# State-space layer: silu and the decays' differences on ScalarE, exponentials in one run, more multiplies on VectorE, the gated norm in two parts

## The chip, the cores and the metric

One core of a Trainium2 chip runs the whole program. The metric is the device time in microseconds, the median of several runs. TensorE (PE) does the matmuls, with weight loads (PEld) beside them; VectorE (DVE), ScalarE (ACT) and GpSimd (POOL) do elementwise work; SyncE (SP) issues most of the DMAs.

## The reference

A trunk of two layers over 512 tokens of width 1024, all in f32. Layer 0 mixes by pooling and chunked attention, layer 1 by a Mamba-2 state-space layer; a mixture of experts follows each. The change is in layer 1's mixer:

```python
zxbcdt = h @ w_in                                   # 512x1024 by 1024x6176
z, xbc, dt = jnp.split(zxbcdt, ...)                 # 2048, 4096, 32 columns
conv = sum(xp[:, tap:tap + s] * conv_w[tap] for tap in range(4))
xbc = jax.nn.silu(conv + conv_b)
xs, Bm, Cm = jnp.split(xbc, ...)                    # 32 heads of 64; 8 groups, state 128
dt = softplus(dt + dt_bias);  x_dt = xs * dt
a_cs = cumsum(dt * -exp(A_log))                     # within a chunk
seg = exp(where(tril, a_cs[l] - a_cs[s], -inf))     # decay between two tokens
y_diag = einsum(Cm, Bm, seg, x_dt)
states = einsum(Bm, exp(a_cs[-1] - a_cs), x_dt)     # one state per chunk, scanned over chunks
y = y_diag + einsum(Cm, prev, exp(a_cs)) + xs * D_skip
g = (y * silu(z)) grouped by 8                      # 256 columns in a group
g = g * rsqrt(mean(g * g) + EPS) * norm_w
out = g @ w_out
```

## The kernel before

`odd_mixer` is the state-space layer. Its loop runs over the 8 groups `g`, with a ninth turn that finishes group 7. Tokens lie along the free axis (512), and are cut in 4 chunks of 128 for the scan (index `cq`).

In each turn PE runs six **dense blocks** of 24 matmuls, in the order `b`, `c`, `x0`, `x1`, `z0`, `z1`. A dense block multiplies the 1024 inputs by 128 columns of `w_in`, with operand and weight each split in a high and a low half (three products). The weights' halves are made two blocks ahead by `wsplit`: ACT copies the high half (L111), and a subtraction makes the low half (L112) on the engine that a string names in turn; for this layer the string is `LO["o"] = "GVV"`, so that every third block's low half is POOL's.

Behind a block of `b`, `c` or `x` comes `conv`: Identity with scale and bias on ACT (L1584), three taps on DVE (L1587), and silu as Tanh on ACT (L1590) with a multiply-add on DVE (L1591). `zgate` does the same for `z` (L1680, L1681). `decay(g, cq)` reads a row of cumulated logs by DMA into `lb`, takes four differences with a minimum on DVE (L1620), an Exp on ACT (L1622) and a mask multiply (L1623, alternately POOL and DVE) and leaves `ms`. `xtok` turns `x` by eight transposes on PE into `pxd` (L1637), multiplies by `dt` on DVE (`xdt`, L1640) and by the decay to the chunk's end on POOL (`xw`, L1643). One group later, `states` multiplies `xw` by `btk` (`pst`, L1651) behind the `b` block and scans the chunks (`prev`), `ymm` makes the outputs' two parts `pyd` (L1670, from `ms` and `xdt`) and `pyo` (L1674), and `assemble` joins them (`yy`, `yt` L1689, POOL's sum L1691, `gT` L1692), squares them and sums them into `gsum` (L1699, POOL). `gnorm` norms two groups at once, after each second turn: two matmuls (`pgn`, L1705), one step on DVE, Ln and Exp on ACT, three steps on DVE, a broadcast on POOL and a scaling of `gT` on DVE (L1721).

Between groups DVE also works on two vectors of the conditioning (`ada`, L202, 128x2048 a step), as many steps a group as `OFILL` says. A static scheduler orders each engine's instructions by priority and by what they need; no engine leaves its order at run time. After the mixer comes the output projection (`so`, L457 to L459), whose operands are `gT`.

Of the kernel before, what the change touches and what calls it, by code (L numbers as in the profile page):

```python
# [9 lines left out]
F32 = mybir.dt.float32  # L10
# [10 lines left out]
P = 128  # L21
# [37 lines left out]
HEAD = 1  # L59
NTMP = 3  # L60
TAIL = 2
FILL = (0, 1, 5, 0, 1, 0, 1, 1, 1, 2, 1, 0, 0, 1, 0, 5, 4, 0, 0, 1, 1, 1, 4, 0, 12)
OFILL = (4, 0, 5, 4, 4, 0, 3, 4)
LO = {"v": "V", "e": "VVG", "m": "V", "o": "GVV", "s": "VV"}
FPOOL = (0,)
# [11 lines left out]
def trunk_kernel(ctx, tc, x, c, ada_w, ada_b, norm1_w, norm2_w, mix_w_in, pool_w, pool_scale,  # L77
# [1377 lines left out]
    def odd_mixer(layer, prev):  # L1455
        with ExitStack() as es:
# [25 lines left out]
            with ExitStack() as es2:  # L1482
# [94 lines left out]
                def tmp(name):  # L1577
                    return gp.tile([P, T], F32, tag="tmp", name=name, bufs=NTMP)

                def conv(kind, ch, bufs, between=None):  # L1580

                    p = dense.next(between)
                    a = gp.tile([P, T], F32, tag=f"cv{kind}", name=f"cv{kind}{ch}", bufs=bufs)
                    S.activation(a, p, AF.Identity, bias=cb[:, ch:ch + 1], scale=cw[:, 3, ch:ch + 1])  # L1584
                    for tap in (2, 1, 0):
                        sh = 3 - tap
                        V.scalar_tensor_tensor(a[:, sh:], p[:, :T - sh], cw[:, tap, ch:ch + 1], a[:, sh:], op0=ALU.mult,  # L1587
                                               op1=ALU.add)
# [25 lines left out]
                def decay(g, cq):  # L1614

                    lb = gp.tile([P, 4, P], F32, tag="lb", name=f"lb{g}{cq}", bufs=2)
                    SP.dma_start(lb, dap(acd, (32 * cq + 4 * g) * P, [[0, P], [1, 4 * P]]))
                    ms = gp.tile([P, 4, P], F32, tag="ms", name=f"ms{g}{cq}", bufs=3)
                    for h in range(4):
                        V.tensor_scalar(ms[:, h, :], lb[:, h, :], acs[:, cq, 4 * g + h:4 * g + h + 1], 0.0,  # L1620
                                        op0=ALU.subtract, op1=ALU.min)
                    S.activation(ms, ms, AF.Exp)  # L1622
                    (V if cq % 2 else GP).tensor_mul(ms, ms, gs[g]["cbm"][:, cq, None, :].to_broadcast([P, 4, P]))  # L1623
                    gs[g]["ms", cq] = ms

                def xtok(g):
# [5 lines left out]
                    for c2 in range(2):  # L1632
# [5 lines left out]
                        for e in range(2):  # L1638
# [3 lines left out]
                            if cq < NT - 1:  # L1642
                                GP.tensor_mul(xw[:, cq], xdt[:, cq], dec[:, cq, hs, None].to_broadcast([P, 4, 64]))  # L1643

# [32 lines left out]
                def zgate(g, q):  # L1677
                    pz = dense.next()
                    z = gs[g]["z", q] = gp.tile([P, T], F32, tag="zt", name=f"zt{g}{q}", bufs=2)
                    S.activation(z, pz, AF.Tanh, scale=0.5)  # L1680
                    V.scalar_tensor_tensor(z, z, 1.0, pz, op0=ALU.add, op1=ALU.mult)  # L1681

                def assemble(g, q):
# [7 lines left out]
                    GP.tensor_add(y[:, P:], y[:, P:], t[:, P:])  # L1691
                    V.tensor_mul(gT[2 * g + q], y, d["z", q])  # L1692
                    if q == 0:
# [7 lines left out]
                def gnorm(g0):  # L1701
# [5 lines left out]
                    v = tmp(f"gv{g0}")  # L1707
                    V.tensor_scalar(v, p, 1.0 / 1024, EPS, op0=ALU.mult, op1=ALU.add)
                    y = tmp(f"gy{g0}")
                    S.activation(y, v, AF.Ln)  # L1710
                    S.activation(y, y, AF.Exp, scale=-0.5)
                    t = tmp(f"gt{g0}")
                    V.tensor_mul(t, y, y)
                    V.scalar_tensor_tensor(t, t, -0.25, v, op0=ALU.mult, op1=ALU.mult)
                    V.scalar_tensor_tensor(y, t, 0.75, y, op0=ALU.add, op1=ALU.mult)
                    for q in range(2):
# [10 lines left out]
                for g in range(G + 1):  # L1727
# [12 lines left out]
                    if g:  # L1740
                        ymm(g - 1, 0)
                        ymm(g - 1, 1)
                        decay(g - 1, 3)
                    if d is not None:
                        d["x", 0] = conv("x", 2 * g, 3)
                    if g:
                        ymm(g - 1, 2)
                        ymm(g - 1, 3)
                    if d is not None:
                        d["x", 1] = conv("x", 2 * g + 1, 3)  # L1750
                    if g:
                        assemble(g - 1, 0)
                        assemble(g - 1, 1)
                    if d is not None:
                        if g == 0:
                            next(dt)
                            zgate(g, 0)
                            next(dt)
                        cbt(g)
                        if g:  # L1760
                            zgate(g, 0)
                        decay(g, 0)
                        zgate(g, 1)
                        xtok(g)
                        decay(g, 1)
                        decay(g, 2)
                        for _ in range(OFILL[g]):
                            if fill:
                                next(fill.pop(0), None)
                    if g == G - 1:  # L1770
# [75 lines left out]
```

## Time and profile before

| | |
|---|---|
| median of 3 runs | 1091.51 us (1089.97 to 1093.85) |
| the profiled execution | 1090.3 us, span 1088.6 us, mean granted clock 0.959 |
| busy: PE, DVE, ACT, POOL | 91%, 65%, 36%, 26% of the span |
| the state-space layer's loop | about 440 to 830 us of the span |

Busy shares are means over two layers of unlike work; what the layer's engines do must be read from its own stretch. The rows that the prediction reads stand two sections below.

### The profile page before, as it was taken

What the parts mean: (1) busy time and instruction counts of PE and PEld (TensorE: products, weight loads), DVE (VectorE), ACT (ScalarE), POOL (GpSimd) and SP (SyncE); (2) the same over time, 40 slices, a digit from 0 to 9 for tenths busy, and PEclk for the clock granted to TensorE, in tenths of its full rate; (3) what the DMA queues carried; (4) which work ended last, traced back from release to release, by engine and by line L of the source; (5) the groups of instructions that cost most, each with busy time, mean ns of one, the idle gap of its engine ahead of it and who ended that gap; (6) DMA issues with size and microseconds to landing.
All of it is one profiled execution on the core that took longest, in us unless ns stands there. A gap on an engine that the chain in (4) does not pass through costs nothing. (4 is left out here: it accounts for less than half of the span.)

```text
span 1088.6 us, 15997 instructions
## 1 busy us (share of the span) xinstructions
PE 988.3 (91%) x5700; PEld 727.1 (67%) x5700; DVE 712.5 (65%) x1607; ACT 389.9 (36%) x753; POOL 283.1 (26%) x324
## 2 busy tenths in 40 slices
PE   5889998896999997998899998999979997998994
PEld 4576555685666657787677786777857876665653
DVE  3523434445656767779898987977976655654874
ACT  4333533323223235333344333445323334222242
POOL 3002110204221045221433624234231005231133
PEclk9899999997999998999899999999989998899998
DMA  9688867696799979447653666445346754799977
GB/s 331 215 282 314 291 225 275 248 358 234 270 399 414 410 177 357 110 131 214 212 155 99 186 218 194 117 121 169 88 136 206 277 188 162 248 412 413 407 253 181
DMA packets 137840, 263.88 MB, mean 242 GB/s; under 512 B 17555, under 2 KB 79975, under 8 KB 132632
## 3 DMA queue, kind: packets, MB, share of 16 engines
q1 hardware_dynamic: 126760, 235.36, 61.8%
q0 software_dynamic: 8928, 20.97, 7.4%
q10 hardware_dynamic: 2064, 6.42, 1.5%
q8 instruction: 49, 0.80, 0.3%
q14 instruction: 39, 0.32, 0.1%
HBM read 254.15 MB, written 20.11 MB: 252 GB/s over the span
## 5 line engine op out<-in xcount | busy, mean ns | idle before, releaser
L1063 PE MATMUL ph<-w,xT 128*64 128x256 f32 (+1 forms) x1152 | 132.3, 374 | 1.3 <-DVE xT L1047 1.1
L1063 PEld LDWEIGHTS ph<-w,xT 128*64 128x64 f32 x1152 | 86.4, 139 | 52.7 <-ACT xT L1049 9.5
L1030 POOL DMA_INDIRECT xg<-xnd,toks x32 | 32.3, 1008 | 152.6 <-PE pxt L1042 117.4
L1084 PE MATMUL pyy<-w,hidT 128*64 128x512 f32 x272 | 65.9, 605 | 2.2 <-ACT hidT L1076 2.2
L1065 ACT ACTIVATE th<-ph 128x128 f32<-128x128 f32 x34 | 9.4, 278 | 155.3 <-PE pht L1074 138.2
L1049 ACT ACTIVATE xT<-pxt,mc 128x128 f32<-128x128 f32 x136 | 51.2, 457 | 17.5 <-DVE xgovt L1264 7.6
L1620 DVE TENSOR_SCALAR ms<-lb,acs 128x128 f32<-128x128 f32 x128 | 44.8, 400 | 15.1 <-PE pyd L1670 10.9
L1089 DVE SCALAR_TENSOR_TENSOR y<-pyy,wsl,gate 128x512 f32<-128x512 f32 x68 | 48.0, 742 | 9.5 <-DMA yd<-y 7.9
L1042 PE MATMUL pxt<-ident,xg 128*128 128x128 f32 x272 | 37.8, 284 | 15.1 <-DVE mi L1281 8.6
L1047 DVE TENSOR_SCALAR xT<-pxt,mc 128x128 f32<-128x128 f32 x136 | 46.6, 404 | 1.4 <-PE pxt L1042 1.4
L1066 DVE SCALAR_TENSOR_TENSOR th<-th,ph 128x128 f32<-128x128 f32 x34 | 9.7, 287 | 57.5 <-ACT th L1065 57.5
L1042 PEld LDWEIGHTS pxt<-ident,xg 128*128 128x128 f32 x272 | 34.4, 195 | 15.6 <-issue 15.3
L1115 DVE TENSOR_TENSOR x<-x,pyc 128x512 f32<-128x512 f32 x48 | 30.4, 682 | 19.0 <-DMA x<-yd,row 14.7
L1623 POOL TENSOR_TENSOR ms<-ms,cbm 128x512 f32<-128x512 f32 x16 | 25.5, 1605 | 61.4 <-DVE cbm L1607 47.7
L1210 POOL DMA_INDIRECT x<-yd,row x16 | 25.4, 1586 | 47.0 <-DVE y L1089 20.4
L1587 DVE SCALAR_TENSOR_TENSOR cvx<-pdx,cw,cvx 128x511 f32<-128x511 f32 (+2 forms) x48 | 35.5, 739 | 1.0 <-ACT cvx L1584 1.0
L202 DVE SCALAR_TENSOR_TENSOR ada<-ada,ccol,ada 128x2048 f32<-128x2048 f32 x14 | 35.5, 2533 | 0.2
L1084 PEld LDWEIGHTS pyy<-w,hidT 128*64 128x64 f32 x272 | 16.5, 136 | 26.0 <-issue 19.4
L492 DVE TENSOR_TENSOR sor<-sor,gate 128x1024 f32<-128x1024 f32 x16 | 20.5, 1281 | 18.8 <-DMA sor<-in_ssm_w_out_dram 18.7
L1651 PE MATMUL pst<-xw,btk 128*128 128x256 f32 x48 | 16.5, 466 | 15.3 <-POOL xw L1643 15.3
L1107 PE MATMUL pyc<-yh,yot 128*128 128x512 f32 x96 | 27.4, 417 | 3.2 <-DVE yot L1097 3.2
L1622 ACT ACTIVATE ms<-ms 128x512 f32<-128x512 f32 x32 | 20.2, 630 | 23.9 <-DVE ms L1620 23.1
(1079 smaller groups left out, 2752.1 us busy)
## 6 DMA issues: line engine op xcount, KB each, us to landing
w<-in_moe_w_dram SPq DMA_DIRECT2D x192, 512.0 KB
ada<-in_ada_w_dram SPq DMA_DIRECT2D x40, 1024.0 KB
yd<-y SPq DMA_DIRECT2D x22, 512.0 KB
ada<-in_ada_w_dram SPq DMA_DIRECT2D x16, 512.0 KB
wx<-in_ssm_w_in_dram SPq DMA_DIRECT2D x16, 512.0 KB
wz<-in_ssm_w_in_dram SPq DMA_DIRECT2D x16, 512.0 KB
lb<-acd SPq DMA_DIRECT2D x32, 256.0 KB
sor<-in_ssm_w_out_dram SPq DMA_DIRECT2D x16, 512.0 KB
```

Source lines behind the costliest of these rows:

```text
L202: a = eng.scalar_tensor_tensor(ws[k], ws[k], ccol[:, k:k + 1], ws[k - 1], op0=ALU.mult, op1=ALU.add)
L1030: d = GP.indirect_dma_start(out=xg, out_offset=None, in_=xnd[:, :], in_offset=bass.IndirectOffsetOnAxis(ap=idx, axis=0), bounds_check=T - ...
L1042: PE.transpose(p[:, q, :], xv[:, 4 * hf + q, :], ident)
L1047: V.tensor_scalar(xT[:, k, :], p[:, q, :], a, b, op0=ALU.mult, op1=ALU.add)
L1049: S.activation(xT[:, k, :], p[:, q, :], AF.Identity, bias=b, scale=a)
L1063: PE.matmul(ph[64 * j:64 * j + 64, n:n + h, :], xT[:, k, 64 * j:64 * j + 64], w13[n][:, :, k, :], start=k == 0, stop=k == KD - 1, skip_gro ...
L1084: PE.matmul(py[64 * j:64 * j + 64], hT[:, 64 * j:64 * j + 64], w2[:, s], start=True, stop=True, skip_group_check=True)
L1089: V.scalar_tensor_tensor(y[:, s], py, self.wsl[:, slot:slot + 1], self.gate2[:, s], op0=ALU.mult, op1=ALU.mult)
L1107: PE.matmul(p, part[2][:, i * P:(i + 1) * P], part[hf][:, q * 512:(q + 1) * 512], start=not sums and n + q == 0, stop=stop and n == len(pa ...
L1115: V.tensor_add(xst["x"][i][:, s], xst["x"][i][:, s], p)
L1587: V.scalar_tensor_tensor(a[:, sh:], p[:, :T - sh], cw[:, tap, ch:ch + 1], a[:, sh:], op0=ALU.mult, op1=ALU.add)
L1620: V.tensor_scalar(ms[:, h, :], lb[:, h, :], acs[:, cq, 4 * g + h:4 * g + h + 1], 0.0, op0=ALU.subtract, op1=ALU.min)
```

## The change

It does the following in the layer's loop.

- Silu is one ACT operation (`AF.Silu`) for all blocks from the first `z` block's second half on; the first group's `b`, `c`, `x0`, `x1` and first `z` keep Tanh and multiply. `in_order` chains Silu, Exp and Ln of the loop in the order in which they are written.
- The decays' differences are made by ACT: Relu of (bias minus input), then Exp with scale -1. `ms` has 4 buffers instead of 3. All four chunks of a group are made together in `exps`, between `ymm(g - 1, 3)` and the conv of `x1`; the mask multiplies are apart, in `masked`, behind `xtok`.
- `xw` is DVE's, and so are all low halves of the layer's weights.
- `gnorm` is a generator: the matmuls, Ln and Exp of a pair run ahead of `exps` of the group after, the rest behind the conv of `x1`. The norm's three DVE steps are written another way, and since `z`'s silu isn't doubled any more, its mean is taken by 1/256.
- The shared temporary tile `tmp` has 2 buffers instead of 3.

```diff
-NTMP = 3
+NTMP = 2
-LO = {"v": "V", "e": "VVG", "m": "V", "o": "GVV", "s": "VV"}
+LO = {"v": "V", "e": "VVG", "m": "V", "o": "V", "s": "VV"}
...
+                def in_order(a):
+
+                    if acts:
+                        tc.add_manual_dep(a.ins, acts[-1].ins.name, NOSYNC, reason="in_order")
+                    acts.append(a)
...
+                    if acts:
+                        in_order(S.activation(a, a, AF.Silu, scale=2.0))
+                        return a
                     t = tmp(f"cvt{ch}")
                     S.activation(t, a, AF.Tanh)
                     V.scalar_tensor_tensor(a, t, 1.0, a, op0=ALU.add, op1=ALU.mult)
...
-                    ms = gp.tile([P, 4, P], F32, tag="ms", name=f"ms{g}{cq}", bufs=3)
+                    ms = gs[g]["ms", cq] = gp.tile([P, 4, P], F32, tag="ms", name=f"ms{g}{cq}", bufs=4)
                     for h in range(4):
-                        V.tensor_scalar(ms[:, h, :], lb[:, h, :], acs[:, cq, 4 * g + h:4 * g + h + 1], 0.0,
-                                        op0=ALU.subtract, op1=ALU.min)
-                    S.activation(ms, ms, AF.Exp)
+                        S.activation(ms[:, h, :], lb[:, h, :], AF.Relu, scale=-1.0,
+                                     bias=acs[:, cq, 4 * g + h:4 * g + h + 1])
+                    in_order(S.activation(ms, ms, AF.Exp, scale=-1.0))
+
+                def exps(g):
+
+                    if g > 2 and g % 2:
+                        norm.append(gnorm(g - 3))
+                        next(norm[-1])
+                    for cq in range(NT):
+                        decay(g, cq)
+
+                def masked(g, cq):
+
+                    ms = gs[g]["ms", cq]
                     (V if cq % 2 else GP).tensor_mul(ms, ms, gs[g]["cbm"][:, cq, None, :].to_broadcast([P, 4, P]))
-                    gs[g]["ms", cq] = ms
...
-                                GP.tensor_mul(xw[:, cq], xdt[:, cq], dec[:, cq, hs, None].to_broadcast([P, 4, 64]))
+                                V.tensor_mul(xw[:, cq], xdt[:, cq], dec[:, cq, hs, None].to_broadcast([P, 4, 64]))
...
+                    if acts:
+                        in_order(S.activation(z, pz, AF.Silu))
+                        return
                     S.activation(z, pz, AF.Tanh, scale=0.5)
                     V.scalar_tensor_tensor(z, z, 1.0, pz, op0=ALU.add, op1=ALU.mult)
...
-                    S.activation(y, v, AF.Ln)
-                    S.activation(y, y, AF.Exp, scale=-0.5)
-                    t = tmp(f"gt{g0}")
-                    V.tensor_mul(t, y, y)
-                    V.scalar_tensor_tensor(t, t, -0.25, v, op0=ALU.mult, op1=ALU.mult)
-                    V.scalar_tensor_tensor(y, t, 0.75, y, op0=ALU.add, op1=ALU.mult)
+                    in_order(S.activation(y, v, AF.Ln))
+                    in_order(S.activation(y, y, AF.Exp, scale=-0.5))
+                    yield
+                    V.scalar_tensor_tensor(v, v, -0.5, y, op0=ALU.mult, op1=ALU.mult)
+                    V.tensor_mul(v, v, y)
+                    V.scalar_tensor_tensor(y, v, 1.5, y, op0=ALU.add, op1=ALU.mult)
...
                         ymm(g - 1, 1)
-                        decay(g - 1, 3)
...
                         ymm(g - 1, 2)
                         ymm(g - 1, 3)
+                    if d is not None and g:
+                        exps(g)
                     if d is not None:
                         d["x", 1] = conv("x", 2 * g + 1, 3)
+                    while norm:
+                        run(norm.pop())
...
                         if g:
                             zgate(g, 0)
-                        decay(g, 0)
                         zgate(g, 1)
                         xtok(g)
-                        decay(g, 1)
-                        decay(g, 2)
+                        for cq in range(NT):
+                            masked(g, cq)
```

The scheduler moves instructions on each engine. On ACT, around group 3's second `x` block, the Exps (L1622), Tanh (L1590) and Identity (L1584) of before stood so:

```order
L1622 ACTIVATE ms30_6074<-ms30_6074 128x512
L1622 ACTIVATE ms31_6136<-ms31_6136 128x512
L1590 ACTIVATE cvt6_5951<-cvx6_5946 128x512
L1622 ACTIVATE ms32_6145<-ms32_6145 128x512
L111 ACTIVATE b4h_6040<-wb4_5966 128x1024
L1584 ACTIVATE cvx7_5997<-pdx31_5972,cb_130,cw_124 128x512
L1612 ACTIVATE btk3_6036<-pbt3_6032 128x384
L1590 ACTIVATE cvt7_6002<-cvx7_5997 128x512
L111 ACTIVATE c4h_6083<-wc4_6038 128x1024
```

and of the change (Exp is L1633, Identity L1592, Silu L1598; L1739 is the norm's Exp):

```order
L111 ACTIVATE b4h_6042<-wb4_5959 128x1024
L1739 ACT_TABLE_LOAD
L1739 ACTIVATE gy0_5924<-gy0_5924 128x512
L1633 ACTIVATE ms30_5929<-ms30_5929 128x512
L1633 ACTIVATE ms31_5937<-ms31_5937 128x512
L1633 ACTIVATE ms32_5945<-ms32_5945 128x512
L1633 ACTIVATE ms33_5953<-ms33_5953 128x512
L1592 ACTIVATE cvx7_5990<-pdx31_5965,cb_130,cw_124 128x512
L1623 ACTIVATE btk3_6038<-pbt3_6034 128x384
L111 ACTIVATE c4h_6075<-wc4_6040 128x1024
L1598 ACT_TABLE_LOAD
L1598 ACTIVATE cvx7_5990<-cvx7_5990 128x512
```

The four Exps now stand in one run ahead of the Identity of `x1` (`cvx7`), where `ms33` was not yet among them; two loads of function tables stand in the piece, one ahead of the norm's Exp and one ahead of the Silu. On DVE, behind group 3's `xtok`, the multiplies `xdt` (L1640) stood so before:

```order
L1640 TENSOR_TENSOR xdt3_6115<-pxd30_6117,dtk_4656 128x256 x2
L1640 TENSOR_TENSOR xdt3_6115<-pxd31_6126,dtk_4656 128x256
L1681 SCALAR_TENSOR_TENSOR zt31_6112<-zt31_6112,pdz31_6087 128x512
L1640 TENSOR_TENSOR xdt3_6115<-pxd31_6126,dtk_4656 128x256
L215 TENSOR_TENSOR adab11_5051<-pada11_6152,adab11_5051 128x512
L204 TENSOR_SCALAR ada120_6173<-ada120_6173,ccol_94 128x2048
L202 SCALAR_TENSOR_TENSOR ada121_6175<-ada121_6175,ccol_94,ada120_6173 128x2048
```

and of the change (`xdt` is L1662, `xw` L1665, the norm's scaling L1749):

```order
L1662 TENSOR_TENSOR xdt3_6106<-pxd30_6108,dtk_4656 128x256 x2
L1749 SCALAR_TENSOR_TENSOR gT0_5077<-gT0_5077,vcol_123,gb01_6003 128x512 x2
L1714 TENSOR_TENSOR yt20_6009<-pyo20_5858,eb2_5656 128x384
L1714 TENSOR_TENSOR yt21_6017<-pyo21_5859,eb2_5656 128x384
L1665 TENSOR_TENSOR xw3_6107<-xdt3_6106,dec_4658 128x256 x2
L1662 TENSOR_TENSOR xdt3_6106<-pxd31_6117,dtk_4656 128x256 x2
L1665 TENSOR_TENSOR xw3_6107<-xdt3_6106,dec_4658 128x256
L215 TENSOR_TENSOR adab11_5059<-pada11_6129,adab11_5059 128x512
L204 TENSOR_SCALAR ada120_6150<-ada120_6150,ccol_94 128x2048
L112 TENSOR_TENSOR x40l_6165<-wx40_6073,x40h_6164 128x1024
L202 SCALAR_TENSOR_TENSOR ada121_6152<-ada121_6152,ccol_94,ada120_6150 128x2048
```

`xw` has come onto DVE between the parts of `xdt`, two scalings of the norm and two `yt` stand among them, and the low half `x40l` follows the ada step; the multiply of `z`'s silu (L1681) is gone. On PE, at the end of the loop, the output projection's matmuls (`so`) between the last norm's two `pgn` were these before, with group 7's last products among them:

```order
L1705 MATMUL pgn6_7723<-gsum6_7516,ones_74 64x512
L457 MATMUL so00_7772<-sow0h_7785,gs0_7789 128x512
L458 MATMUL so00_7772<-sow0l_7786,gs0_7789 128x512
L459 MATMUL so00_7772<-sow0h_7785,gs0_7789 128x512
L1670 MATMUL pyd70_7671<-ms73_7687,xdt7_7608 64x128 x2
L1670 MATMUL pyd71_7672<-ms73_7687,xdt7_7608 64x128 x2
L457 MATMUL so01_7773<-sow0h_7785,gs0_7789 128x512
L458 MATMUL so01_7773<-sow0l_7786,gs0_7789 128x512
L459 MATMUL so01_7773<-sow0h_7785,gs0_7789 128x512
...
L457 MATMUL so00_7772<-sow1h_7819,gs1_7823 128x512
L1705 MATMUL pgn6_7723<-gsum7_7712,ones_74 64x512
L458 MATMUL so00_7772<-sow1l_7820,gs1_7823 128x512
```

and of the change:

```order
L1696 MATMUL pyo70_7608<-cvc31_7315,prev7_7594 128x128
L1696 MATMUL pyo71_7609<-cvc31_7315,prev7_7594 128x128
L1733 MATMUL pgn6_7649<-gsum6_7476,ones_74 64x512
L457 MATMUL so00_7697<-sow0h_7710,gs0_7714 128x512
L458 MATMUL so00_7697<-sow0l_7711,gs0_7714 128x512
L459 MATMUL so00_7697<-sow0h_7710,gs0_7714 128x512
...
L457 MATMUL so11_7700<-sow0h_7710,gs0_7714 128x512
L458 MATMUL so11_7700<-sow0l_7711,gs0_7714 128x512
L1733 MATMUL pgn6_7649<-gsum7_7638,ones_74 64x512
L459 MATMUL so11_7700<-sow0h_7710,gs0_7714 128x512
```

Group 7's products now all come ahead of the first `pgn`, and 11 matmuls of the projection stand between the two where 25 stood.

## Rows read from the trace of the kernel before

**Rows 1.** The page, busy us, share of the span and instructions of each engine.

```profile
PE 988.3 (91%) x5700; PEld 727.1 (67%) x5700; DVE 712.5 (65%) x1607; ACT 389.9 (36%) x753; POOL 283.1 (26%) x324
```

**Rows 2.** Windows: length, busy of PE, PEld, DVE, ACT, POOL, granted clock, DMA share, GB/s.

```profile
440.00:830.00 390.00, 363.28 (x1834) 286.33 (x1833) 331.89 (x530) 151.51 (x218) 129.03 (x90) 0.97 0.51 151
858.00:885.00 27.00, 27.00 (x121) 22.35 (x120) 14.90 (x15) 7.71 (x11) 0.00 (x0) 1.00 0.54 193
```

**Rows 3.** Waits of PE, 440 to 830 us: total, times, longest.

```profile
PE pst L1651 <- POOL xw L1643: 15.3, 8, 6.4
PE pgn L1705 <- POOL gsum L1699: 3.8, 3, 1.6
PE pdx L449 <- DVE cvb L1587: 3.1, 2, 2.9
PE pacs L1550 <- DVE dt L1545: 2.4, 1, 2.4
PE pyo L1674 <- DVE prev L1659: 1.3, 1, 1.3
```

**Rows 4.** Windows at a granted clock of 0.50: the last of four, and their sum.

```profile
798.70:805.50 6.80, 4.28 (x20) 3.21 (x22) 4.68 (x11) 0.38 (x1) 2.20 (x3) 0.50 0.70 243
sum 20.40, PE 16.95 PEld 13.25 DVE 18.25 ACT 1.88 POOL 3.95; mean PE 4.24 PEld 3.31 DVE 4.56 ACT 0.47 POOL 0.99
```

**Rows 5.** Lines, 440 to 830 us: count, busy us, mean ns, idle before.

```profile
L1620 DVE TENSOR_SCALAR ms<-lb,acs 128x128 f32<-128x128 f32 x128 | 44.8, 400 | 15.1 <-PE pyd L1670 10.9 <-DMA lb<-acd 4.2
L1643 POOL TENSOR_TENSOR xw<-xdt,dec 128x256 f32<-128x256 f32 x24 | 26.6, 1139 | 3.2 <-DVE xdt L1640 3.2
L1640 DVE TENSOR_TENSOR xdt<-pxd,dtk 128x256 f32<-128x256 f32 x32 | 11.6, 409 | 0.1
L1591 DVE SCALAR_TENSOR_TENSOR cvx<-cvt,cvx 128x512 f32<-128x512 f32 x16 | 13.3, 830 | 1.1 <-ACT cvt L1590 1.1
L1681 DVE SCALAR_TENSOR_TENSOR zt<-zt,pdz 128x512 f32<-128x512 f32 x16 | 10.7, 675 | 0.5 <-ACT zt L1680 0.5
L1689 DVE TENSOR_TENSOR yt<-pyo,eb 128x384 f32<-128x384 f32 x16 | 8.2, 544 | 0.0
```

**Rows 6.** One line's instructions: a low half made by DVE, ns.

```profile
L112 DVE TENSOR_TENSOR z10l<-wz,z10h x1: 1214/1214/1214, 498.9 to 498.9; 128x1024 fp32r<-128x1024 f32 x1
```

**Rows 7.** Timeline of DVE and POOL in two places: start, us, engine, line.

```profile
617.76 6.84 POOL L1643 TENSOR_TENSOR xw<-xdt,dec 128x256 f32<-128x256 f32 x3
618.93 5.20 DVE L202 SCALAR_TENSOR_TENSOR ada<-ada,ccol,ada 128x2048 f32<-128x2048 f32 x2
455.42 2.39 POOL L112 TENSOR_TENSOR z01l<-wz,z01h 128x1024 fp32r<-128x1024 f32 x1 [13.45 <-ACT z01h L111]
455.43 2.46 DVE L1539 TENSOR_SCALAR dt<-dt 128x128 f32<-128x128 f32 x1
```

**Rows 8.** Lines of ACT by form, whole span, 128x128.

```profile
L1049 ACT ACTIVATE xT<-pxt,mc 128x128 f32<-128x128 f32 x136 | 51.2, 457 | 17.5 <-DVE xgovt L1264 7.6 <-DVE r L1282 5.5 <-PE pxt L1042 4.3
L1528 ACT ACTIVATE dt<-dt 128x128 f32<-128x128 f32 x1 | 0.3, 312 | 0.1
L1555 ACT ACTIVATE cdec<-pacs 128x128 f32<-128x128 f32 x1 | 0.3, 262 | 0.0
```

**Rows 9.** Lines of ACT, 440 to 830 us.

```profile
L1622 ACT ACTIVATE ms<-ms 128x512 f32<-128x512 f32 x32 | 20.2, 630 | 23.9 <-DVE ms L1620 23.1
L1711 ACT ACT_TABLE_LOAD x4 | 5.1, 1283 | 0.1
```

**Rows 10.** Timeline of PE at the end of the loop; in brackets idle before.

```profile
801.23 2.93 PE L1651 MATMUL pst<-xw,btk 128*128 128x256 f32 x6 [6.37 <-POOL xw L1643]
808.12 1.07 PE L1705 MATMUL pgn<-gsum,ones 128*64 128x512 f32 x2
810.01 0.66 PE L1670 MATMUL pyd<-ms,xdt 128*64 128x128 f32 x8
816.59 1.07 PE L1705 MATMUL pgn<-gsum,ones 128*64 128x512 f32 x2 [1.39 <-POOL gsum L1699]
```

More of the change, by code (lines that the diff above doesn't have):

```diff
@@ L1578, in tmp @@
                     return gp.tile([P, T], F32, tag="tmp", name=name, bufs=NTMP)
+                acts, norm = [], []
+                def in_order(a):
+                    if acts:
+                        tc.add_manual_dep(a.ins, acts[-1].ins.name, NOSYNC, reason="in_order")
+                    acts.append(a)
                 def conv(kind, ch, bufs, between=None):
@@ L1691, in assemble @@
                     GP.tensor_add(y[:, P:], y[:, P:], t[:, P:])
-                    V.tensor_mul(gT[2 * g + q], y, d["z", q])
+                    if g + q:
+                        V.tensor_mul(gT[2 * g + q], y, d["z", q])
+                    else:
+                        V.scalar_tensor_tensor(gT[2 * g + q], y, 0.5, d["z", q], op0=ALU.mult, op1=ALU.mult)
                     if q == 0:
@@ L1707, in gnorm @@
                     v = tmp(f"gv{g0}")
-                    V.tensor_scalar(v, p, 1.0 / 1024, EPS, op0=ALU.mult, op1=ALU.add)
+                    V.tensor_scalar(v, p, 1.0 / 256, EPS, op0=ALU.mult, op1=ALU.add)
                     y = tmp(f"gy{g0}")
-                    S.activation(y, v, AF.Ln)
-                    S.activation(y, y, AF.Exp, scale=-0.5)
-                    t = tmp(f"gt{g0}")
-                    V.tensor_mul(t, y, y)
-                    V.scalar_tensor_tensor(t, t, -0.25, v, op0=ALU.mult, op1=ALU.mult)
-                    V.scalar_tensor_tensor(y, t, 0.75, y, op0=ALU.add, op1=ALU.mult)
+                    in_order(S.activation(y, v, AF.Ln))
[4 more added lines that the diff above has]
+                    V.scalar_tensor_tensor(y, v, 1.5, y, op0=ALU.add, op1=ALU.mult)
                     for q in range(2):
@@ L1758, in odd_mixer @@
                             next(dt)
+                            exps(g)
                         cbt(g)
@@ L1774, in odd_mixer @@
                         moe.weights(W8)
-                    if g and g % 2 == 0:
-                        gnorm(g - 2)
+                    if g == G:
+                        run(gnorm(G - 2))
             moe.open(xd, "left")
```

## The prediction

> **What bounds the kernel now.** I began with the busy line of the page [rows 1]: PE works 91% of the span, DVE 65%, ACT 36%. That is a mean over a whole two-layer trunk, and the change sits in one stage, so I cut out the Mamba stage, 440 to 830 us. There DVE is busy 331.89 of 390 us, PE 363.28, ACT 151.51 and POOL 129.03 [rows 2]: DVE is nearly as full as PE and ACT is not. PE is still the bound, so a gain can come only from its idle time. The view of PE's waits names that: 15.3 us of `pst` waiting for `xw` on POOL, 3.8 of `pgn` for `gsum`, 3.1 of a dense block for a conv tile on DVE, 2.4 at the start for `dt` and 1.3 for `prev`; together 25.9 us [rows 3]. After some of them TensorE falls from its 2.4 GHz level to 1.2: in four stretches the granted clock is 0.50, with PE busy 16.95 us [rows 4]. The same work at full clock would take half, so 8.5 us are lost, 2.1 of them in the last stretch (4.28 busy), at the stage's end, and 6.3 in the three before. The ceiling of the change is 25.9 + 8.5 = 34.4 us. A gain should pass on whole: in the output projection behind, PE works 27.00 of 27 us and nothing else waits [rows 2].
>
> Why is `xw` late? It is three multiplies on POOL behind DVE's `xdt`. POOL's mean is 1139 ns where DVE's like multiply takes 409 [rows 5], and at 617.76 POOL's three stood for 6.84 us while DVE ran two 128x2048 ada steps of together 5.20 [rows 7].
>
> **The change on DVE.** The prices are in [rows 5, 6], POOL's 2.39 in [rows 7]. Gone: 128 subtract/min (44.8); 28 of 32 multiplies that finish the conv's silu, at most 0.83 each (23.2; group 0 keeps four); 15 of 16 for `z` (10.1). Added: 24 `xw` at 0.409 (9.8), and 16 lower halves at 1.214, which POOL did at 2.39 (19.5). 331.9 - 44.8 - 23.2 - 10.1 + 9.8 + 19.5 = 283.1 of 390. The subtract row also shows contention: its mean is 400 ns, and it goes.
>
> **On ACT.** The subtractions come as 128 Relu on 128x128. No row shows a Relu from SBUF; bounds are 262 and 457 ns, the two ACT forms of that shape that read PSUM; between lies one from SBUF to SBUF at 312 [rows 8], which I take because it moves between the same memories: 39.9 us (33.5 to 58.5). Silu takes Tanh's place at its price of 630 ns for a 128x512 tile (the Exp row shows the same). By the order, twelve more table loads stand in the layer, at 1.283 each [rows 9]: 15.4. ACT goes to 151.5 + 39.9 + 15.4 = 207 of 390: room on the whole, so the question is only where it stands in line.
>
> The Trainium skill (ScalarE: Activation LUTs, Rules for kernel authors) speaks against this part: Relu and min belong on VectorE, and each switch of function set is to be budgeted at about 2.7 us. The trace's load takes 1.283 with 0.1 us idle before it [rows 9]; by the Trainium skill's figure the twelve would be an estimated 32 us, and ACT 224 of 390.
>
> **On POOL.** 129.0 - 26.6 (`xw`) - 16 x 2.4 (38) leaves about 64. The mask multiplies on it, still every other one, only lose competition.
>
> **Term by term on PE.**
> 1. `pst` in the middle: 15.3 less the tail's 6.37 = 8.9 [rows 3, 10]. `xw` follows `xdt` on the same engine at 0.41; before the first `pst` lies a whole dense block (24 matmuls at 27.00/121 = 0.223, 5.35 us [rows 2]). Where a 2.6 us ada step slips between, the block still covers it. **8.9**, at worst half.
> 2. The dense block's 3.1: DVE loses 48.8 us of work. **3.1**, at worst nothing.
> 3. `pgn` in the middle, 3.8 less 1.39 at the end: its matmuls move a group later, when `gsum` is long done. **2.4**.
> 4. The start, 2.4 us for `dt`: one of its short DVE steps took 2.46 us, just while POOL subtracted [rows 7]; now the subtraction stands on DVE itself for 1.2. **1.0** of 2.4.
> 5. The half clock after these waits: **6.3** if they go, nothing if they stay.
> 6. The tail. `pst` of group 7 waits 6.37 us from 794.86 [rows 10]. Now behind `xtok`'s transposes stand on DVE two `xdt` (0.8), two scalings (1.4 at the price of `z`'s like multiply), two `yt` (1.1) and one `xw` (0.4) [rows 5]: 3.7. From `pst` to the end of the y products PE needs about 6.4 (it took 6.9 from 801.23 to `pgn`, partly at half clock); the last `gsum` comes 5.9 behind its products now (810.67 to 816.59). So the second `pgn` comes 3.7 + 6.4 + 5.9 = 16.0 us behind `xtok`, against 21.7 now: 5.7 sooner. But as the order shows, 11 instead of 25 output matmuls are done by then: 14 x 0.223 = 3.1 less. 2.6 remain; the first `pgn` now waits some 3 us for group 6's `gsum`, which may cost up to 1.7 of clock. **1.0**, from 0 to 2.6.
> 7. New waits: **-4.0**. The silu of `x1` stands behind all Exps. From the start of `x1`'s block: 8 Relu left (2.5), four Exp (2.5) and a load (1.3), Identity (0.6), three taps (2.5), load and silu (1.9) = 11.3; with the norm's Ln, Exp and their loads 3.8 more: 15.1. `xtok` comes after three blocks, 16.1. The slack of 1 to 5 us is eaten where an ada step (2.6) and two lower halves (2.4) stand between the taps. I count 1 us in each of four groups (the bounds: 0, and 8 groups of 4.7, the slower rival).
>
> 8.9 + 3.1 + 2.4 + 1.0 + 6.3 + 1.0 - 4.0 = 18.7. The profiled execution took 1090.3 us (span 1088.6), so 1071.6 on its own terms; the median of the runs, 1091.51, lies 1.2 higher: **1073**. All else (norm in fewer steps, `tmp` with two buffers instead of three) I cost at nothing: the norm's chain is covered by dense blocks, and `tmp` loses its users `cvt`, so the two left are asked for less often; if that cover fails, POOL's broadcasts hold up scaling, which only the tail feels.
>
> **The rivals.** *(B) DVE stays late.* 283 of 390 is still 73%, in order, with ada steps of 2.6 us; the 16 lower halves are cheaper than on POOL but no longer beside DVE. If half of terms 1, 2 and 5 stays (9.2), we get 1082 to 1083. For it speaks that now, with DVE at 85%, the waits come just where ada stands [rows 7]; against it that 48.8 us leave. *(C) Everything goes*, tail too, with no new wait: 18.7 + 4.0 + 1.6 + some of the 1.7 and `dt`'s 1.4, and `pyo`'s 1.9: 28 to 30, about 1062. *(D) The waits only move*: PE's banks and weights let it run two blocks ahead, so that what it does not lose at `pst` it loses at `xtok`: within 3.3 us of 1091.5. *(E) Slower: ACT's line.* Relu writes into a `ms` slot that is free only when the y products of the group before have read it, so ACT can't run ahead; Identity and silu of `x1` queue behind. If `xtok` waits 3.0 us in each of 8 groups and TensorE then falls to half clock (6.3 us for three stretches now, some 1.7 to 2.1 each), it costs 8 x 4.7 = 37.6 against gains of 22.7: 1106. It decides from (22.7 + 3.3)/8 = 3.3 us per group on. For it: slack of 1 us in the groups with the norm; against: ACT idles half of the stage, and the slack is 5 elsewhere. By the Trainium skill's 2.7 us per switch (same page and section), two switches on this path would add an estimated 2.8 us per group; the 0.1 us of idle time [rows 9] does not show it.
>
> **How the numbers follow.** Forecast (gain 11 to 26, so 1065 to 1080) 0.52; B 0.18; C 0.10; D 0.08; E 0.12. Runs of before spread over 3.9 us, so I hold 0.3% (3.3 us) to be what can be told from no change. Faster: 0.52 + 0.18 + 0.10 = 0.80; same 0.08; slower 0.12. The range leaves out D and E (0.20) and reaches from C to beyond B: 1060 to 1087.
>
> **What the profile after would show.** Right: DVE about 283 and ACT about 207 in the stage; no `pst` wait for `xw` in groups 0 to 6; no half clock before the tail; Relu near 0.31; `xtok`'s transposes waiting for ACT some 4 us in all. Wrong: `pxd` waiting for the silu of `x1` over 3 us a group (E), `pst` still waiting for a DVE that runs ada (B), or a Relu at 0.45, which would add 8 x 0.14 = 1.1 us to `x1`'s path in each group.

## The result, and the profile after

The changed kernel takes 1078.05 us in the median of 4 runs (1074.8 to 1078.15), against 1091.62 us before: a ratio of 0.9876, 95% interval 0.9855 to 0.9898. That is 13.6 us less where the prediction's sum gave 18.7; it lies in the forecast case's range (1065 to 1080). The profiled execution took 1078.06 us, span 1076.4.

The layer's loop is best read in pieces that mean the same in both kernels: up to the `b` block of group 1, from there to that of group 7, from there to the last `pgn`, and the rest. In these windows of the kernel before, columns as in [rows 2], the pieces are 36, 278, 63 and 271 us long:

```profile
440.00:476.00 36.00, 33.63 (x173) 28.21 (x172) 25.57 (x52) 13.19 (x20) 4.36 (x2) 1.00 0.40 107
476.00:754.00 278.00, 261.65 (x1325) 205.42 (x1323) 245.74 (x384) 108.59 (x157) 104.61 (x72) 0.98 0.55 164
754.00:817.00 63.00, 55.17 (x290) 43.22 (x289) 52.05 (x86) 22.81 (x33) 17.41 (x15) 0.95 0.41 129
817.00:1088.00 271.00, 243.02 (x1507) 174.09 (x1505) 164.22 (x416) 87.38 (x193) 58.19 (x82) 0.94 0.78 276
```

The same windows of the changed kernel, and under them its whole loop:

```profile
440.00:481.00 41.00, 37.04 (x174) 30.63 (x173) 26.39 (x54) 13.70 (x22) 0.00 (x0) 0.92 0.41 108
481.00:740.00 259.00, 251.14 (x1321) 201.42 (x1320) 208.11 (x271) 155.14 (x281) 51.94 (x38) 1.00 0.60 178
740.00:804.00 64.00, 54.64 (x283) 41.86 (x281) 45.14 (x65) 27.79 (x49) 11.55 (x10) 0.92 0.38 122
804.00:1076.00 272.00, 242.81 (x1517) 174.52 (x1516) 163.70 (x416) 87.52 (x193) 58.12 (x82) 0.95 0.77 275
440.00:816.00 376.00, 354.83 (x1824) 283.60 (x1823) 286.04 (x398) 203.62 (x358) 64.61 (x50) 0.98 0.53 156
```

The middle gained 19 us: PE's idle time there fell from 16.4 to 7.9 (length less busy), and its busy time by 10.5. Of these, 6.3 are the half clock counted from [rows 4] (the granted clock went from 0.98 to 1.00), and 1.1 are four `pgn` that now stand in the end piece; the other 3 are not accounted for. The start lost 5: in the profiled execution two stretches of 3.3 and 3.5 us at 1.2 GHz stand there, where before had none. The end lost 1 (its stretch at 1.2 GHz grew from 6.8 to 10.2 us), and what lies behind passed on all but 1. The waits of PE, 440 to 830 us, which answer to [rows 3]:

```profile
PE pst L1673 <- DVE xw L1665: 7.8, 3, 6.6
PE pxd L1659 <- ACT cvx L1598: 3.2, 1, 3.2
PE pgn L1733 <- POOL gsum L1727: 2.7, 2, 1.5
PE pacs L1550 <- DVE dt L1545: 2.6, 1, 2.6
PE pyo L1696 <- ACT zt L1703: 2.1, 3, 1.4
PE pdtt L1521 <- DVE dt L1518: 1.4, 1, 1.4
PE pdx L449 <- DVE cvb L1595: 1.1, 1, 1.1
```

Of `pst`'s 15.3 us 7.8 are left, and 6.6 of them are the one wait at the end of the loop. The prices of the new operations, as lines of the loop (they answer to [rows 5, 8, 9]):

```profile
L1631 ACT ACTIVATE ms<-lb,acs 128x128 f32<-128x128 f32 x128 | 40.0, 391 | 5.9 <-DMA lb<-acd 5.9
L1598 ACT ACT_TABLE_LOAD x7 | 9.0, 1283 | 20.2 <-DVE cvx L1595 20.2
L1665 DVE TENSOR_TENSOR xw<-xdt,dec 128x256 f32<-128x256 f32 x24 | 9.3, 417 | 0.0
```

Why does `xw` still wait at the end? Three timelines of that place tell it, of PE, POOL and DVE (start, us, operation, in brackets the idle time before):

```profile
788.37 2.90 PE L1673 MATMUL pst<-xw,btk 128*128 128x256 f32 x6 [6.62 <-DVE xw L1665]
```
```profile
772.93 3.31 POOL L1646 TENSOR_TENSOR ms<-ms,cbm 128x512 f32<-128x512 f32 x2 [41.74 <-DVE cbm L1618]
782.29 0.80 POOL L1746 PARTITION_BROADCAST gb<-gy  x1 [6.05 <-issue]
784.71 0.80 POOL L1746 PARTITION_BROADCAST gb<-gy  x1 [1.62 <-DVE gT L1749]
792.44 1.94 POOL L1716 TENSOR_TENSOR yy<-yy,yt 128x384 f32<-128x384 f32 x2 [6.93 <-DVE prev L1678]
```
```profile
775.66 1.13 DVE L1743 SCALAR_TENSOR_TENSOR gy<-gv,gy 128x512 f32<-128x512 f32 x1
783.13 1.42 DVE L1749 SCALAR_TENSOR_TENSOR gT<-gT,vcol,gb 128x512 f32<-128x512 f32 x2 [2.69 <-POOL gb L1746]
784.46 0.75 DVE L1662 TENSOR_TENSOR xdt<-pxd,dtk 128x256 f32<-128x256 f32 x2
787.81 0.75 DVE L1665 TENSOR_TENSOR xw<-xdt,dec 128x256 f32<-128x256 f32 x2
```

The broadcast's input `gy` is done at 776.8, POOL's mask multiplies end at 776.2, and the broadcast starts only at 782.3. DVE stands in its order at the scaling that needs it, with `xdt` and `xw` behind. Six microseconds pass in which POOL shows nothing ("issue"). The experiments turn on this gap.

### The profile page after: what moved, and what is told of

Its sections match the earlier page's. It is cut to its first block, busy times and chain, and to the rows that moved or that the text cites. A ratio compares the mean times of both kernels' runs of the same rounds, so it can differ in the third digit from the quotient of the medians.

```text
span 1076.4 us, 15960 instructions
## 1 busy us (share of the span) xinstructions
PE 975.1 (91%) x5700; PEld 718.9 (67%) x5700; DVE 667.7 (62%) x1476; ACT 440.6 (41%) x893; POOL 219.9 (20%) x284
## 5 line engine op out<-in xcount | busy, mean ns | idle before, releaser
L1115 DVE TENSOR_TENSOR x<-x,pyc 128x512 f32<-128x512 f32 x48 | 30.5, 684 | 22.6 <-DMA x<-yd,row 18.3
L1631 ACT ACTIVATE ms<-lb,acs 128x128 f32<-128x128 f32 x128 | 40.0, 391 | 5.9 <-DMA lb<-acd 5.9
L1716 POOL TENSOR_TENSOR yy<-yy,yt 128x384 f32<-128x384 f32 x16 | 20.0, 1255 | 102.2 <-DVE yt L1714 81.2
L1084 PEld LDWEIGHTS pyy<-w,hidT 128*64 128x64 f32 x272 | 16.5, 136 | 26.0 <-issue 19.4
L492 DVE TENSOR_TENSOR sor<-sor,gate 128x1024 f32<-128x1024 f32 x16 | 19.5, 1223 | 21.4 <-DMA sor<-in_ssm_w_out_dram 21.4
L168 PE MATMUL pada<-ada,ccol 128*32 128x512 f32 x192 | 24.9, 600 | 1.0 <-DMA ada<-in_ada_w_dram 1.0
```

Of the source, the lines that this page charges most:

```text
L1084: PE.matmul(py[64 * j:64 * j + 64], hT[:, 64 * j:64 * j + 64], w2[:, s], start=True, stop=True, skip_group_check=True)
L1115: V.tensor_add(xst["x"][i][:, s], xst["x"][i][:, s], p)
L1631: S.activation(ms[:, h, :], lb[:, h, :], AF.Relu, scale=-1.0, bias=acs[:, cq, 4 * g + h:4 * g + h + 1])
```

## The experiments

They were timed in three batches, each beside runs of the kernel before on the same chip (its medians there: 1092.61, 1092.67 and 1093.18 us). The changed kernel was timed in the comparison above alone, so a difference to it is one between batches, whose medians of before lie up to 1.6 us apart. Three theories stood first. L: the middle gained because DVE carries less. X: because `xw` left POOL. H: because the low halves left POOL. What the others (S, T, W, Q, C) say stands where they are tested.

**One part of the change undone.** `e1_xw_pool`:

```diff
-                                V.tensor_mul(xw[:, cq], xdt[:, cq], ...)
+                                GP.tensor_mul(xw[:, cq], xdt[:, cq], ...)
```

> The changed kernel with xw back on POOL alone. Theory L (the middle's gain comes from DVE's lighter load): POOL has little else to do now, three multiplies at 1.14 us are covered by the b block of 5.35 us, so the middle keeps most of its gain: time 0 to +4 us on the changed kernel, pst waiting for xw up to 4 us in groups 0 to 6. Theory X (the engine of xw is what mattered): the pst waits of before (8.9 us in the middle) and the half clock behind them (6.3) come back: +10 to +15 us.

Measured: 1097.66 us, 1.0049 of before (1.0027 to 1.0070), so 19.6 us worse than the changed kernel; no theory had expected so much. `e2_lo_gvv`:

```diff
-LO = {..., "o": "V", ...}
+LO = {..., "o": "GVV", ...}
```

> The changed kernel with every third low half of the weights back on POOL. Theory S (the loss at the start comes from the two first low halves now on DVE): the start, from the layer's first block to the first block of group 1, regains 4 to 5 us; the middle, where DVE is no longer late, neither gains nor loses more than 2; together -5 to -2 us. Theory H (taking the halves off POOL is itself a part of the middle's gain, by contention with DVE): the middle loses 4 to 8 us, so the whole is 0 to +4.

Measured: 1096.88 us, 1.0036 (1.0011 to 1.0062): 18.8 us worse, where S expected a gain and H at most a loss of 4. `e3_diff_dve`:

```diff
-                        S.activation(ms[:, h, :], lb[:, h, :], AF.Relu, scale=-1.0, bias=acs[...])
-                    in_order(S.activation(ms, ms, AF.Exp, scale=-1.0))
+                        V.tensor_scalar(ms[:, h, :], lb[:, h, :], acs[...], 0.0, op0=ALU.subtract, op1=ALU.min)
+                    in_order(S.activation(ms, ms, AF.Exp))
```

> The changed kernel with the decays' differences back on DVE (subtract and min, then Exp), everything else as changed. Theory L: DVE gets some 35 to 45 us of work back and is at about 320 to 330 us of the stage again, so convs and xw come late: +5 to +12 us, with pst or dense blocks waiting for DVE. Theory X: xw stays on DVE, so the gain stays: within 2 us of the changed kernel.

Measured: 1079.82 us, 0.9882 (0.9842 to 0.9922): within noise of the changed kernel's time. `e4_tanh`, with the factors of the norm set back to a doubled `z`:

```diff
-                    if acts:
-                        in_order(S.activation(a, a, AF.Silu, scale=2.0))
-                        return a
...
-                    if acts:
-                        in_order(S.activation(z, pz, AF.Silu))
-                        return
```

> The changed kernel with silu as Tanh on ACT and a multiply-add on DVE in all blocks, the rest as changed. Theory L: DVE gets about 33 us of work back, ACT loses the eight function-table loads ahead of Silu: +3 to +8 us. Theory X: within 2 us. If the loads ahead of Silu were a cost on the path of x1, it would be faster by 1 to 3 us instead.

Measured: 1079.17 us, 0.9871 (0.9832 to 0.9911): the same again. In these two, DVE is busy 320.0 and 318.5 us of the 390, against 295.9 in the changed kernel, and nothing clear of noise is lost: 1.8 and 1.1 us in the medians, 5 and 4 at the upper ends of the intervals, against the changed kernel's ratio. So DVE's load, taken back one half at a time, is not what made the middle slow, and L falls as it was put for the differences (5 to 12 us); for the silu (3 to 8) its lower end is not excluded. Both halves together were not taken back.

What `e1_xw_pool` lost shows in POOL's line in group 5's place (first fence) and in PE's waits (second: a row of the timeline and the sum over the loop):

```profile
691.55 3.31 POOL L1646 TENSOR_TENSOR ms<-ms,cbm 128x512 f32<-128x512 f32 x2 [26.83 <-DVE cbm L1618]
701.28 0.80 POOL L1746 PARTITION_BROADCAST gb<-gy  x1 [6.41 <-issue]
703.70 0.80 POOL L1746 PARTITION_BROADCAST gb<-gy  x1 [1.62 <-DVE gT L1749]
711.54 0.60 POOL L1665 TENSOR_TENSOR xw<-xdt,dec 128x256 f32<-128x256 f32 x1 [7.04 <-DVE cvb L1595]
```
```profile
712.20 1.22 PE L1673 MATMUL pst<-xw,btk 128*128 128x256 f32 x2 [6.38 <-POOL xw L1665]
PE pst L1673 <- POOL xw L1665: 28.7, 6, 11.8
```

`xdt` was ready (DVE's first two parts end at 704.2), yet `xw` starts 7.0 us behind the broadcast. POOL takes some 6 us here to go from an elementwise operation to a broadcast (6.05 and 6.41), and some 7 to go back (6.93 and 7.04). The Trainium skill (GPSIMD Engine Reference, Instruction dispatch) has a cost of that size: the first call of a freshly loaded kernel pays about 6 us (it gives 5.95) for loading its code, and no instruction in the profile shows it. The traces agree in the size; that each such change on POOL is a load of code is a guess, and no run here shows what POOL does in the gap. Call it theory P that these gaps are what PE pays for: what matters is whether something that PE waits for stands in POOL's order next to a broadcast.

The lengths of the turns say the same. A turn runs from the first matmul of one group's `b` block to the next group's, as the views of these tiles give them (the start from 440 us, the end to the last `pgn`); `pst` of group g stands in turn g + 1, and the norm's second part runs in turns 3, 5 and 7 of the changed order, ahead of `xw` of those groups:

| us | start | 1 | 2 | 3 | 4 | 5 | 6 | end |
|---|---|---|---|---|---|---|---|---|
| before | 35.9 | 45.7 | 51.6 | 42.0 | 46.2 | 47.3 | 45.2 | 63.2 |
| after | 40.9 | 41.0 | 44.4 | 42.8 | 43.1 | 42.1 | 45.5 | 64.0 |
| e1, xw on POOL | 37.6 | 41.3 | 46.0 | 42.8 | 50.7 | 41.7 | 54.1 | 70.7 |
| e2, halves on POOL | 36.0 | 45.3 | 41.9 | 42.8 | 51.5 | 46.4 | 51.8 | 66.5 |
| e6, before with halves on DVE | 38.2 | 43.1 | 42.2 | 48.5 | 41.5 | 47.4 | 45.1 | 62.5 |
| e11, broadcasts late | 37.8 | 43.1 | 45.9 | 42.7 | 41.2 | 49.3 | 45.2 | 71.6 |
| e12, the same, xw on POOL ahead of them | 38.3 | 41.4 | 46.0 | 42.7 | 46.8 | 41.6 | 44.5 | 73.5 |

`e1` loses 7.6, 8.6 and 6.7 us in turns 4, 6 and the end, the three with a broadcast ahead of `xw`, and nothing elsewhere in the middle above 1.6. `e2` loses most in turns 4 and 6 too (8.4 and 6.3): there a low half stands on POOL between the two broadcasts, so that the gap is paid there and back once more (first fence: group 3's), and PE waits for `xw` and for `yt`, which stands behind the scalings on DVE (second fence: sums over the loop). It loses 4.3 each in turns 1 and 5, where PE waits 1.7 and 1.2 us for conv tiles and 2.8 for `xw`, and a stretch at 1.2 GHz follows in each.

```profile
615.32 3.27 POOL L112 TENSOR_TENSOR x40l<-wx,x40h 128x1024 fp32r<-128x1024 f32 x1 [9.34 <-issue]
626.30 0.80 POOL L1746 PARTITION_BROADCAST gb<-gy  x1 [7.70 <-issue]
```

```profile
PE pst L1673 <- DVE xw L1665: 9.9, 3, 6.2
PE pyo L1696 <- DVE yt L1714: 9.1, 2, 4.9
```

**One part alone, on the kernel before.** `e5_before_xw_dve` is the edit of `e1` the other way round:

> The kernel before with xw moved to DVE alone. Theory X (the engine of xw is what mattered): 10 to 15 us faster than before. Theory L (DVE's lighter load is what mattered): xw adds 10 us to a DVE that is 85% busy, the pst waits become shorter but others come: 3 to 7 us faster.

Measured: 1093.83 us, 1.0008 (0.9988 to 1.0028). `pst`'s wait fell to 6.2 us, but `pgn` then waited 8.2 and `pdx` 5.7: the waits only moved. X falls, and L, which expected 3 to 7 us here, with it. `e6_before_lo_v` sets the string to "V":

> The kernel before with all low halves on DVE alone. Theory S (start) and theory L: DVE goes up by 19.5 us, the start loses 4 to 5 us, the middle loses too: 4 to 10 us slower than before. Theory H (off POOL is a gain in itself): the start's loss is balanced by the middle, within 3 us.

Measured: 1082.56 us, 0.9905 (0.9879 to 0.9931): ten microseconds from one string, where L and S expected a loss. H is right in its sign, though it expected a change within 3 us. Two rows against [rows 5] show what went with it: in the mean DVE's subtractions took 296 ns instead of 400, and POOL's `xw` 738 instead of 1139, though neither was touched:

```profile
L1620 DVE TENSOR_SCALAR ms<-lb,acs 128x128 f32<-128x128 f32 x128 | 31.8, 296 | 5.2 <-DMA lb<-acd 4.2 <-PE pyd L1670 1.0
L1643 POOL TENSOR_TENSOR xw<-xdt,dec 128x256 f32<-128x256 f32 x24 | 17.2, 738 | 45.8 <-ACT zt L1680 42.2 <-DVE xdt L1640 3.5
```

`e9_before_x0_dve` sets it to "VVVGVV", so that only the eight halves of the first `x` block move:

> The kernel before with only the eight low halves of the first x block moved to DVE; those of the second z block stay on POOL. Theory Q (in POOL's order the next group's first x half stands right ahead of xw, and pst waits through it): these eight give nearly all of the 10 us that all sixteen gave, 7 to 10 us faster than before, and pst's wait for xw in the middle falls to under 3 us. Theory C (POOL's subtractions slow DVE's operations wherever they stand): half of the halves give half, 4 to 6 us.

Measured: 1084.72 us, 0.9924 (0.9898 to 0.9950), 8.5 of the 10 us, and `pst` waited 0.8 us in the middle (7.2 in all, 6.4 at the end). That is what Q, the queue ahead of `xw`, expected; the interval's upper end (5.5 us) leaves room for C. `e10_before_lo_xw` joins the edits of `e5` and `e6`:

> The kernel before with all low halves and xw on DVE, nothing else: ACT's work, the norm and the decays as before. If the two moves off POOL are the change (theory P: it is POOL's line that PE waits through, not DVE's load), 1076 to 1082 us, as the changed kernel. If the silu, Relu and norm parts carry a share beside them, 1083 to 1088.

Measured: 1091.43 us, 0.9986 (0.9958 to 1.0015). The two moves off POOL are not the change: together they give less than the halves alone. Its trace shows two waits in places where `e6` was faster by 7.5 and 5.6 us: `pgn` in turn 4, and `xw` at the end, behind the projection's operands on DVE (L492, 4.22 us for two):

```profile
656.16 1.97 PE L1705 MATMUL pgn<-gsum,ones 128*64 128x512 f32 x2 [4.39 <-POOL gsum L1699]
798.05 2.98 PE L1651 MATMUL pst<-xw,btk 128*128 128x256 f32 x6 [5.26 <-DVE xw L1643]
```

In the changed kernel the norm's matmuls come a group later and wait 2.7 us in all, at the end.

**The start.** `e7_start` puts two halves of group 0 back on POOL:

```diff
+LO = {..., "o": "GVVG" + 44 * "V", ...}
```

> The changed kernel with only the first two low halves that POOL made before in the loop (first x block, second z block of group 0) back on POOL. Theory S: the first b block of group 1 starts 4 to 5 us earlier, at about 476 us, the two stretches at half clock near 445 and 466 us go, and the whole is 3 to 5 us faster than the changed kernel. Rival: the start's loss is a difference between two executions: within 1.5 us.

Measured: 1076.78 us, 0.9838 (0.9813 to 0.9863). The `b` block of group 1 starts at 476.7 us, but with the halves on DVE it started at 475.0 to 478.5 in `e1`, `e3`, `e4`, `e6`, `e8`, `e10`, `e11` and `e12`. The 480.9 of the profiled execution, with its two stretches at 1.2 GHz, is thus mostly that execution's own, and S falls as the cause of the start's loss. In the medians the edit gains 1.3 us, in the ratios 4; with its interval touching the changed kernel's, it is not shown to be faster.

**The end.** `e8_masks` orders POOL's masks of groups 3, 5 and 7 behind the broadcasts:

```diff
...
+                    if casts and cq % 2 == 0:
+                        tc.add_manual_dep(m.ins, casts[-1].ins.name, NOSYNC, reason="masked")
...
```

> The changed kernel with POOL's mask multiplies of groups 3, 5 and 7 behind the norm's broadcasts in POOL's order, not ahead. Theory T (at the end of the loop xw waits on DVE behind scalings that wait for a broadcast, which starts 6 us after POOL's last mask multiply): the broadcast starts right behind its input at about 777 us, DVE comes to xdt as soon as the transposes are done, the 6.6 us wait falls to 1 to 2 us and the half clock behind it shortens: 4 to 7 us faster. Rival W (PE waits for the broadcast's or the masks' late result anyway): the y products wait for the masks instead, within 2 us of the changed kernel.

Measured: 1079.74 us, 0.9880 (0.9855 to 0.9905). POOL's line at the end of the loop:

```profile
778.44 0.81 POOL L1748 PARTITION_BROADCAST gb<-gy  x1 [43.04 <-DVE gy L1745]
781.51 1.10 POOL L1748 PARTITION_BROADCAST gb<-gy  x1 [2.27 <-DVE gT L1751]
789.64 1.70 POOL L1646 TENSOR_TENSOR ms<-ms,cbm 128x512 f32<-128x512 f32 x1 [7.03 <-PE pst L1675]
```

The broadcast now starts with its input, as T said, and `pst` waits 3.2 instead of 6.6. But the mask starts 7.0 us behind the broadcast, and `pyd` waits for it (2.8 in all); dense blocks wait 4.4 for `prev`, 3.3 of it in turn 4. So W: the time stayed. `e11_late` instead moves broadcasts and scalings of a pair behind `xtok` and the masks:

```diff
+                    yield
                     for q in range(2):
                         b = tmp(f"gb{g0}{q}")
...
-                    while norm:
-                        run(norm.pop())
+                    if norm:
+                        next(norm[0])
...
                         for cq in range(NT):
                             masked(g, cq)
+                        while norm:
+                            run(norm.pop())
```

> The changed kernel with the norm's broadcasts and scalings of groups 3, 5 and 7 behind xtok and the masks. Theory T (at the end of the loop xw waits on DVE behind scalings that wait for the broadcast): pst's 6.6 us wait falls to 1 to 2 us, none takes its place because nothing on PE's path needs the scalings: 3 to 7 us faster. Rival W: group 6's sums come later and pgn waits instead: within 2 us.

Measured: 1090.83 us, 0.9987 (0.9962 to 1.0011): the whole gain is gone, which neither T nor W expected. `pst` still waits 5.8 us at the end, with no scaling ahead of it: `xdt` and `xw` now stand on DVE behind the projection's operands (L492 and L112). And the way back now stands ahead of group 7's sum `yy`, which the last norm needs:

```profile
796.46 1.63 POOL L1747 PARTITION_BROADCAST gb<-gy  x1 [5.87 <-issue]
802.29 0.80 POOL L1747 PARTITION_BROADCAST gb<-gy  x1 [4.21 <-DVE gT L1750]
810.76 1.95 POOL L1716 TENSOR_TENSOR yy<-yy,yt 128x384 f32<-128x384 f32 x2 [7.67 <-issue]
```
```profile
815.91 1.97 PE L1733 MATMUL pgn<-gsum,ones 128*64 128x512 f32 x2 [4.31 <-POOL gsum L1727]
```

The end is 7.6 us longer by it (71.6 against 64.0); the other large loss, turn 5 (49.3 against 42.1), holds a wait of `pxd` of 3.95 us for the silu of group 4's `x1`, whose taps stand on DVE behind masks, an ada step and two low halves. `e12_late_xw_pool` adds `xw` on POOL, ahead of the broadcasts:

```diff
-                                V.tensor_mul(xw[:, cq], xdt[:, cq], ...)
+                                xws.append(GP.tensor_mul(xw[:, cq], xdt[:, cq], ...))
...
+                        tc.add_manual_dep(c.ins, xws[-1].ins.name, NOSYNC, reason="cast")
...
```

> The same with xw on POOL, ahead of the broadcasts in POOL's order. Theory P: what cost 19 us when xw alone went back to POOL was the broadcast ahead of it, with 6 us from an elementwise operation to a broadcast and 7 us back; without it pst's 28.7 us of waiting fall to under 12 and the time to within 5 us of the changed kernel. Rival (POOL's multiplies are themselves too slow): still over 10 us slower than the changed kernel.

Measured: 1092.07 us, 0.9996 (0.9973 to 1.0019). `pst`'s wait fell from 28.7 to 5.8 us, as P expected, but the time came only to 14.0 us of the changed kernel, not to 5: by the time alone the rival's forecast came true. Its cause did not: beside `e11`, which has `xw` on DVE (1090.83), `xw` on POOL costs 1.2 us, within noise, and the end waits as in `e11`. The middle settles it: 263.0 us here (turns 1 to 6), 276.6 in `e1`, 258.9 in the changed kernel. So 13.6 of the 17.7 us that `e1` lost there go with the broadcast ahead of `xw`, and not with POOL's speed.

## Why the prediction was right, and where it was not

**The number** held: the middle was forecast at 8.9 + 3.1 + 2.4 + 6.3 - 4.0 = 16.7, and 19 were measured. Its terms one by one: `pst` in the middle fell from 8.9 to 1.2; `pgn` there from 2.4 to nothing; the dense block's 3.1 to 1.1; the three stretches at half clock went; of the new waits (4.0) there came one of 3.2, `pxd` for the silu of a conv tile, and three of together 2.1, `pyo` for the silu of `z`. The terms thus gave 7.7 + 2.4 + 2.0 + 6.3 - 5.3 = 13.1 of the 19. Waits that no term had (`pyo` for `prev`, `pyd` for a mask) gave 1.9, the four `pgn` 1.1, and 3 stay unaccounted for, so that the sum came so near is in part luck. The busy times were right too: DVE 286 (283 forecast), ACT 204 (207), POOL 65 (64). The Relus took 40.0 us of ACT, 39.9 forecast; their mean of 391 ns counts what overlaps. Every one of the loads seen took 1.283, and the 2.7 us that the Trainium skill (ScalarE: Activation LUTs, Rules for kernel authors) budgets per switch do not show here: `e4`, which has none ahead of Silu, was not faster.

**The terms that were off** are those of the loop's start and end. Term 4 gave the start 1.0; `pacs` waits 2.6 where it waited 2.4, so nothing was gained there, and the sign "no half clock before the tail" failed by the two stretches in the start. Term 6 gave the end 1.0, and it lost about 1, which is what the four `pgn` that moved there cost. Its step "`xdt`, two scalings, two `yt`, one `xw`: 3.7" took the scalings as ready to run. They waited 2.69 + 0.34 us for the broadcasts, and with these 3.0 the sum comes to 6.7, where 6.6 were measured. The trace of before had shown it: there, too, the first broadcast of a pair followed an idle POOL, and the prediction took no price from that.

```profile
581.97 1.48 POOL L1718 PARTITION_BROADCAST gb<-gy  x2 [5.78 <-DVE x31l L112]
679.92 1.48 POOL L1718 PARTITION_BROADCAST gb<-gy  x2 [7.62 <-issue]
761.68 2.07 POOL L1718 PARTITION_BROADCAST gb<-gy  x2 [6.92 <-ACT prev L1654]
```

The second shows it best: its input `gy` had been done for 5.6 us. The first's had been done for 1.8; the third's only for 0.6, so this row alone proves nothing. Two figures of the prediction are misread, without weight: rival C has 1.9 us for `pyo` where [rows 3] has 1.3, and sixteen halves at 1.214 are 19.4, not 19.5.

**The reason was partly wrong.** The step that gave the credit to DVE's lighter load (term 2, and rival B) isn't what the runs show: 24.1 us of it (`e3`) or 22.6 (`e4`) could be put back for less than 2 us in the medians. Nor was `xw` late only for its three slow multiplies on POOL: in `e9` they stay there, and 8.5 us come from taking away the low half ahead of them. The other thing that POOL's order decides, whether a gap of 6 to 7 us beside a broadcast falls ahead of `xw`, did not cost in the kernel before, where `xw` stood ahead of the broadcasts; the changed order would have paid it, had `xw` stayed on POOL (`e1`). Rival D, that waits only move, is what happened with `xw` alone (`e5`) and with both moves (`e10`). Rival E did not come: ACT's line made `pxd` wait 3.2 us in all, and `pyo` 2.1.

**Open.** Parts of this change do not add: halves alone -10, `xw` alone +1, both -2, all -13.6, and each of the two taken from the whole +19. What closes the 13 us between `e10` and the changed kernel is among the rest of the change: the norm's later matmuls, DVE's relief as a whole, the exponentials in one run. None was run alone on `e10`, so their shares aren't settled. The waits of `e10` name candidates only: in its middle `pgn` waits 4.6 us, dense blocks 3.8 for conv tiles and `pyd` 3.4 for masks on DVE, where the changed kernel has none, 1.1 and none. No version was shown to beat the changed kernel beyond its interval.

## What to carry to other kernels

Price a change of kind on an engine, not only its operations: look for idle time before the first custom operation and behind the last, and keep what the critical engine waits for out of that neighbourhood. Where an engine looks too full, put part of its work back before crediting the relief; where an edit frees a wait, ask which wait is next in the same turn. In a loop of this kind, undoing one part of a good combination can cost more than the whole had gained.

## What the runs showed of the hardware

POOL's gaps are there in every kernel whose POOL line was read, with no instruction shown: with the input ready, from an elementwise operation to a broadcast 5.6 to 7.8 us, and back 6.7 to 9.3. In `e8` the broadcast had an idle POOL for 43 us and started 0.15 us behind its input, so the gap can pass while POOL has nothing else to do. Two MEMSETs behind a broadcast (`e2`, at 626.95 us) show no gap.

POOL's work slows DVE's and the reverse: with sixteen 2.4 us subtractions off POOL, an untouched DVE operation fell from 400 to 296 ns in the mean. Its median hardly moved (278 and 276 ns); single ones took up to 2.5 us, as long as one of POOL's subtractions, beside which they stood:

```profile
729.87 2.99 DVE L1620 TENSOR_SCALAR ms<-lb,acs 128x128 f32<-128x128 f32 x4 [0.96 <-PE pyd L1670]
730.17 2.42 POOL L112 TENSOR_TENSOR z61l<-wz,z61h 128x1024 fp32r<-128x1024 f32 x1 [14.36 <-ACT z61h L111]
```

And some waits of PE brought a stretch at 1.2 GHz with them: in the middle before three (with 2.9, 2.9 + 1.9 and 0.7 + 1.9 us of idle time just ahead), after none, though `pxd` waited 3.2 us there; in the start after two, behind 1.4 and 2.6 us.
